# The FFN's up projection as a seven-product block multiplication, with the token axis in quarters

## The chip, the cores and the metric

The kernel runs on one core of one Trainium2 chip. The metric is the device time of one execution in microseconds (us); the profile is one execution of the same program. The engines are named as in the profile: PE (matmuls), PEld (PE's weight loads), DVE (vector), ACT (scalar), POOL (GpSimd) and SP, which issues nearly all DMAs.

## The reference

One encoder layer on T = 1088 tokens (1024 of a prompt, 64 of a sample), model width 1024, FFN width 2816 = 22 x 128, all in float32. Two branches (a gated recurrence and differential attention) are mixed, then comes the FFN; the change lies in the last lines:

```
u = x @ w_in                                     # both branches start from here
...
m   = sigmoid(g_hg) * (y_hg @ w_br_hg) + sigmoid(g_da) * (y_da @ w_br_da)
h   = layer_norm(ALPHA * x + m @ w_out)
up  = h @ w_up                                   # 1024 -> 5632 columns, value | gate
c   = causal depthwise conv3(up) + conv_b        # the state's two rows go in front
val, gate = split(c)
out = layer_norm(ALPHA * h + (silu(gate) * val) @ w_down)
```

## The kernel before

Everything is kept transposed: channels on the 128 partitions, tokens on the free axis. A float32 product is made exactly on PE: each operand is split into a high part (a cast on ACT) and a low part (value minus high part, a subtraction on DVE), and each 128-deep step takes three matmuls, (weight high, token high), (weight high, token low) and (weight low, token high), each with its own weight load. A matmul is named by its token part and its weight part: `mm<-hl,whi` is the second of the three. Tiles of weights (`wraw` by DMA, `whi` from ACT at L68, `wlo` from DVE at L69; 128 x 512 each, that is four 128-deep steps of one 128-column tile) rotate through six buffers in this part of the program.

The stages at the end of the program, in order:

- **br_da** (in `mix`): attention outputs `ydh`/`ydl` times w_br_da; eight column tiles, each over three token chunks (`CHUNKS`, 364, 362 and 362 columns), 24 matmuls per chunk (`proj_chunk`, L84).
- **w_out** (in `mix`): mixed branches `mh`/`ml`, chunk by chunk over eight column tiles. Each chunk's layer norm (`layer_norm`: sums on DVE and POOL, squares on ACT, column sums on PE) follows its eighth tile and gives `hh`/`hl`, the FFN's token operand. `s_r` holds h in DRAM for the residual.
- **up** (in `ffn`, `up_proj`): for each f of the 22, a value tile and a gate tile, each over three chunks of 24 matmuls; ACT copies each result to `u` (L942). After the third chunk a convolution follows: one pass on ACT (L948), two on DVE (L950, L952). Then silu on ACT (L958), value times gate on DVE (L959), and the result goes to DRAM (`s_act`). Its first 256 tokens are also split and kept on chip for all 22 f (`a0h`, `a0l`, L960 and L961). An `order` list starts with chunks 0 and 1 of f = 0 and 1, since chunk 2 of h comes last.
- **down** (in `ffn`): four token chunks (256, 288, 288, 256), eight column tiles each, 66 matmuls per tile (L1016). Chunk 0 takes `a0h`/`a0l`; the others load `s_act` again (`araw`, three buffers) and split it into `ah`/`al` (30 buffers each).

All engines run their instructions in program order; the order between stages is set by the tile framework's scheduler, which places instructions by its own simulation.

Of the kernel before, what the change touches and what calls it, by code (L numbers as in the profile page):

```python
# [10 lines left out]
F32 = mybir.dt.float32  # L11
# [24 lines left out]
CHUNKS = ((0, 364), (364, 362), (726, 362))  # L36
LEVELS = (64, 32, 16)
# [8 lines left out]
class K:  # L46
# [52 lines left out]
    def setup_params(self, cp, pp):  # L99
# [14 lines left out]
        with ExitStack() as es:  # L114
# [34 lines left out]
            # lower bound of the forget gate: softmax over the two rows of logits  # L149
# [18 lines left out]
            # lambda on every partition  # L168
# [55 lines left out]
    def store_x(self, gp):  # L224
        """The sum of the parts is x again, for the residual."""
# [20 lines left out]
    def hgrn(self, h, mm, sc, xs, hp, w0=None):  # L246
# [35 lines left out]
        def lvl(B):  # L282
# [16 lines left out]
            if B == 64:  # L299
                # only the blocks' first halves on the partitions, 32 each  # L300
# [34 lines left out]
        # innermost blocks: one reference in the middle, both signs  # L335
# [18 lines left out]
        # decayed keys and queries at the chunk borders  # L354
# [12 lines left out]
        # states  # L367
# [17 lines left out]
        # outputs  # L385
# [693 lines left out]
```

## Time and profile before

| | |
|---|---|
| time, median of 3 runs (lowest to highest) | 2430.59 us (2429.81 to 2436.18) |
| the profiled execution | span 2430.4 us |
| busy: PE, PEld | 2380.3 us (98%), 2327.2 us (96%) |
| busy: DVE, ACT, POOL | 1379.3 us (57%), 1078.4 us (44%), 385.9 us (16%) |
| chain that ended last, by engine | PE 89%, DMA 3%, DVE 2%, ACT 2% |

How to read it: the span is what the profiler saw from the first to the last instruction; here it agrees with the time to 0.2 us. Busy is the share of the span in which an engine worked. The chain is followed back from the last instruction to whatever released it at each step. Matmul records overlap, since they are pipelined: the pace of PE is read from the starts of successive matmuls, not from the length of one.

### The profile page before, as it was taken

How to read it: one execution, taken by the hardware profiler on the slowest of the kernel's cores; microseconds unless marked ns; L12 is line 12 of the kernel's file. 1: busy time of each engine (PE TensorE's matmuls, PEld its weight loads, DVE VectorE, ACT ScalarE, POOL GpSimd, SP SyncE). 2: the span in 40 equal slices, each digit the busy share in tenths (PEclk: the TensorE clock that was granted, in tenths of full speed). 3: DMA queues.
4: the chain of work that ended last, by engine and by line, in shares of the span. 5: the costliest groups of instructions: out<-in, count | busy, mean ns of one | idle time of the engine just before them, and what ended most of it. 6: DMA issues, size and time to landing. Idle time of an engine off the chain costs nothing.

```text
span 2430.4 us, 40166 instructions
## 1 busy us (share of the span) xinstructions
PE 2380.3 (98%) x15528; PEld 2327.2 (96%) x15528; DVE 1379.3 (57%) x2330; ACT 1078.4 (44%) x2108; POOL 385.9 (16%) x519
## 2 busy tenths in 40 slices
PE   8999999999999999999999999999999999999997
PEld 7999999999999999999999999999999999999997
DVE  3666665554666565565567565874444444456665
ACT  3444444443344344344347543454433333355554
POOL 2222222221521121121120000231000000000100
PEclk9999999999999999999999999999999999999999
DMA  4111111111632332332337674642222121287775
GB/s 126 39 40 47 42 43 48 43 45 54 197 82 79 100 92 70 106 92 70 106 87 235 191 234 143 195 128 73 66 62 65 58 65 58 63 232 226 226 211 157
DMA packets 386278, 260.98 MB, mean 107 GB/s; under 512 B 20667, under 2 KB 375895, under 8 KB 386086
## 3 DMA queue, kind: packets, MB, share of 16 engines
q1 hardware_dynamic: 385574, 258.11, 35.9%
q8 instruction: 122, 2.00, 0.3%
q0 software_dynamic: 512, 0.29, 0.1%
q14 instruction: 70, 0.57, 0.1%
HBM read 191.23 MB, written 54.52 MB: 101 GB/s over the span
## 4 chain that ended last, share of the span: by engine, by line
PE 89%; DMA 3%; DVE 2%; ACT 2%; issue 1%; SPq 0%; POOL 0%; POOLq 0%; DVEq 0%; ACTq 0%
PE mm L84 67%; PE mm L1016 8%; PE s L553 3%; PE av L594 2%; DMA araw<-s_act 2%; PE lv L316 1%; PE wt L588 1%; PE nat L242 1%; DMA gb<-s_g 1%; PE o L399 1%; PE o L402 1%; PE avd L642 1%; PE bs L349 1%; PE U L372 1%; ACT whi L68 1%
## 5 line engine op out<-in xcount | busy, mean ns | idle before, releaser
L84 PE MATMUL mm<-x,whi 128*128 128x362 f32 (+1 forms) x3456 | 878.2, 333 | 6.9 <-ACT x L220 5.5
L84 PEld LDWEIGHTS mm<-x,whi 128*128 128x128 f32 x3456 | 613.5, 190 | 12.6 <-ACT x L220 6.1
L69 DVE TENSOR_TENSOR wlo<-wraw,whi 128x512 fp32r<-128x512 f32 x536 | 371.6, 699 | 431.1 <-ACT whi L68 428.5
L84 PE MATMUL mm<-x,wlo 128*128 128x362 f32 (+1 forms) x1728 | 574.3, 333 | 0.0
L68 ACT CAST whi<-wraw 128x512 fp32r<-128x512 f32 x536 | 320.5, 606 | 410.5 <-PE mm L84 304.5
L84 PE MATMUL mm<-hh,wlo 128*128 128x362 f32 (+1 forms) x1056 | 347.0, 329 | 0.0
L84 PE MATMUL mm<-hh,whi 128*128 128x362 f32 (+1 forms) x1056 | 346.3, 329 | 0.0
L84 PE MATMUL mm<-hl,whi 128*128 128x362 f32 (+1 forms) x1056 | 345.9, 328 | 0.0
L84 PEld LDWEIGHTS mm<-x,wlo 128*128 128x128 f32 x1728 | 327.5, 190 | 1.7 <-issue 1.0
L84 PEld LDWEIGHTS mm<-hl,whi 128*128 128x128 f32 x1056 | 199.2, 189 | 0.1
L84 PEld LDWEIGHTS mm<-hh,whi 128*128 128x128 f32 x1056 | 199.1, 189 | 0.1
L84 PEld LDWEIGHTS mm<-hh,wlo 128*128 128x128 f32 x1056 | 198.9, 188 | 0.0
L1016 PE MATMUL mm<-ah,whi 128*128 128x288 f32 (+1 forms) x528 | 154.3, 293 | 1.0 <-ACT ah L1000 0.9
L1016 PE MATMUL mm<-ah,wlo 128*128 128x288 f32 (+1 forms) x528 | 153.7, 292 | 0.0
L1016 PE MATMUL mm<-al,whi 128*128 128x288 f32 (+1 forms) x528 | 153.3, 291 | 0.1
L942 ACT COPY u<-mm 128x364 f32<-128x364 f32 (+3 forms) x176 | 63.3, 386 | 187.5 <-PE mm L84 187.5
L1016 PEld LDWEIGHTS mm<-ah,whi 128*128 128x128 f32 x528 | 99.2, 188 | 1.7 <-ACT ah L1000 1.5
L1016 PEld LDWEIGHTS mm<-al,whi 128*128 128x128 f32 x528 | 99.4, 188 | 0.3 <-DVE al L1001 0.3
L1016 PEld LDWEIGHTS mm<-ah,wlo 128*128 128x128 f32 x528 | 99.3, 188 | 0.2
L553 PE MATMUL s<-B,A 128*128 128x512 f32 (+3 forms) x384 | 87.7, 354 | 2.3 <-ACT E L574 1.6
L950 DVE SCALAR_TENSOR_TENSOR c<-u,par,c 128x1090 f32<-128x1090 f32 x44 | 59.6, 1355 | 47.3 <-ACT c L948 46.2
L480 POOL TENSOR_TENSOR KL<-kT,B 64x512 fp32r<-64x512 f32 x32 | 49.3, 1540 | 217.9 <-DVE B L479 193.3
(301 smaller groups left out, 4144.7 us busy)
## 6 DMA issues: line engine op xcount, KB each, us to landing
wraw<-w_down SPq DMA_DIRECT2D x160, 256.0 KB, 3.6
wraw<-w_in SPq DMA_DIRECT2D x144, 256.0 KB, 2.9
wraw<-w_up SPq DMA_DIRECT2D x88, 256.0 KB, 2.9
wraw<-w_br_hg SPq DMA_DIRECT2D x48, 256.0 KB, 3.5
wraw<-w_out SPq DMA_DIRECT2D x48, 256.0 KB, 3.1
s_act<-c SPq DMA_DIRECT2D x22, 384.0 KB, 2.3
A<-A SPq DMA_DIRECT2D x64, 128.0 KB, 2.6
araw<-s_act SPq DMA_DIRECT2D x44, 144.0 KB, 3.6
```

The costliest lines, as they stand in the source:

```text
L68: nc.scalar.copy(hi[:, :kn, :], raw[:, :kn, :])
L69: nc.vector.tensor_tensor(lo[:, :kn, :], raw[:, :kn, :], hi[:, :kn, :].bitcast(F32), ALU.subtract)
L84: nc.tensor.matmul(ps[:, :cw], l, r[:, :cw], start=(k == 0 and i == 0), stop=(k == n - 1 and i == 2))
L242: nc.tensor.transpose(ps[:m, i * P:(i + 1) * P], src[:, c * P:c * P + m], self.ident)
L316: nc.tensor.matmul(ps[:m, ch * 64:(ch + 1) * 64], st, mv, start=True, stop=True)
L349: nc.tensor.matmul(ps[:, i, :], X[:, sl], Qp[:, sl], start=True, stop=True)
L480: G.tensor_tensor(kl[r], kT[r, sl], b[r, m, :].bitcast(F32), ALU.subtract)
L553: nc.tensor.matmul(dst[:, kc * 512:kc * 512 + kw], A[i // 2][:, p, m, qc], B[kc][:, m, :kw], start=(p == 0), stop=(p == 1))
L594: self.last_av = nc.tensor.matmul(av[:, i % n4, :], wT[:, kb, :], vn[:, kb, :], start=(kb == 0), stop=(kb == i))
L942: S.copy(u[:, b + off:e + off], ps[:, b - c0:e - c0])
L950: V.scalar_tensor_tensor(c[:, :W - 2], u[:, 1:W - 1], par[:, self.o_w1 + j:self.o_w1 + j + 1], c[:, :W - 2], ALU.mult, ALU.add)
L1016: nc.tensor.matmul(ps[:, :cw], l, r[f][:, :cw], start=(f == 0 and i == 0), stop=(f == NF - 1 and i == 2))
```

## The change

For each f the up projection is one product of a 2 x 2 block matrix of weights (rows: value tile, gate tile; columns: first and second half of the contraction, four 128-deep steps each) and a 2 x 2 block matrix of tokens (rows: the halves of the contraction; columns: two token quarters of 272). It is made with seven block products in place of eight. The token quarters are paired (0, 2) and (1, 3), so each f has two "lanes", c = 0 and c = 1, with 7 x 12 matmuls of 272 columns each. The operands are sums and differences: four of the weights (`wsum`, on POOL) for each f, four of the tokens (t1 to t4) for each pair. Pair 0's token sums are made on POOL; of pair 1's, t1 and t2 on DVE and t3 and t4 on POOL. The products are accumulated in three PSUM banks per lane, and DVE adds them up while it evacuates them. br_da and w_out also run in quarters, w_out pair by pair; for f = 0 and 1, lane 0 of both comes first and lane 1 after it, with the weights made again. Only f = 20 and 21 keep `a0h`/`a0l`; down's chunk 0 loads the other twenty. The rest of the diff renames comments, moves the set-up of `qbd`, sends the last head's attention output through DRAM like the others, and moves pools.

```
     def split_w(self, raw, kn=4):
+        hi, lo = self.wtile("whi", F32R), self.wtile("wlo", F32R)
+        nc.scalar.copy(hi[:, :kn, :], raw[:, :kn, :])
+        nc.vector.tensor_tensor(lo[:, :kn, :], raw[:, :kn, :], hi[:, :kn, :].bitcast(F32), ALU.subtract)
...
+    def seven_weights(self, w, c1, c2, early=False):
...
+        def comb(x, y, op):
+            t = self.wtile("wsum", F32)
+            G.tensor_tensor(t, x, y, op)
+            return t
+        a11 = load(0, c1)
+        yield self.split_w(a11)
+        if early:
+            yield self.split_w(load(4, c1))
+        a21 = load(0, c2)
+        s1 = comb(a21, load(4, c2), ALU.add)
+        yield self.split_w(s1)
+        if early:
+            a11 = load(0, c1)
+        s2 = comb(s1, a11, ALU.subtract)
+        yield self.split_w(s2)
+        a12 = load(4, c1)
+        if not early:
+            yield self.split_w(a12)
+        yield self.split_w(comb(a11, a21, ALU.subtract))
+        yield self.split_w(comb(a12, s2, ALU.subtract))
+        yield self.split_w(load(4, c2))
...
+    def seven_tokens(self, out, za, zb, tile, eng):
...
+        eng.tensor_tensor(t1, b12, b11, ALU.subtract)
+        self.split_tokens(out, "t1", t1, tile)
...
+    def seven_products(self, lanes, tmp, order="1562734"):
...
+            for (gen, x, put), d in zip(lanes, st):
+                w = ws[gen] = ws[gen] if gen in ws else next(gen)
+                bank = {"1": "A", "2": "A", "5": "C", "3": "C"}.get(n, "B")
...
+                if n in "156":
+                    t = d[n] = tmp.tile([P, QW], F32, tag=f"p{n}", name=self.nm("p" + n), bufs=2)
+                    if n == "1":
+                        S.copy(t, ps)
+                    else:
+                        V.tensor_tensor(t, ps, d["1"], ALU.add)
+                    continue
+                row, half, other = {"2": (0, 0, None), "7": (1, 1, "5"), "3": (0, 1, "6"), "4": (1, 0, "1")}[n]
+                for sl, dst in put(row, half):
+                    if other is None:
+                        S.copy(dst, ps[:, sl])
+                    else:
+                        V.tensor_tensor(dst, ps[:, sl], d[other][:, sl], ALU.add)
...
-            self.layer_norm(z, cw, self.o_l1g, self.o_l1b, lnp, zp, CW, ci == 2, done)
+                self.layer_norm([z[k // 4][:, k % 4, :] for k in range(KT)], QW, self.o_l1g, self.o_l1b, lnp, lp,
+                                pi == 1)
...
+            self.xop.append(self.seven_tokens(ops, zz[0], zz[1], optile, V if pi else G))
...
+        for c in range(2):
+            self.seven_products([(weights(f, c == 1), self.xop[c], put(us[f], c)) for f in range(2)], up,
+                                "1256734" if c else "1562734")
...
+        for f in range(2, NF):
+            u, w = new_u(f), weights(f)
+            self.seven_products([(w, self.xop[c], put(u, c)) for c in range(2)], up)
+            conv(f, u)
...
-            if ci == 0:
-                ah, al = a0h, a0l
...
+                if ci == 0 and f >= KEEP:
+                    hi, lo = a0h[f], a0l[f]
+                else:
+                    raw = ap.tile([P, DW], F32, tag="araw", name=self.nm("araw"), bufs=8)
```

The instructions on DVE around one f in the middle of the up projection, before (`wlo` is a weight tile's low part, `c` the convolution's tile, `u` the up projection's result, `a0l` the kept low part):

```order
L950 SCALAR_TENSOR_TENSOR c_17505<-u_17408,par,c_17505 128x1090
L952 SCALAR_TENSOR_TENSOR c_17505<-u_17408,par,c_17505 128x1090
L69 TENSOR_TENSOR wlo_17829<-wraw_17826,whi_17828 128x512
L69 TENSOR_TENSOR wlo_17835<-wraw_17832,whi_17834 128x512
L950 SCALAR_TENSOR_TENSOR c_17605<-u_17408,par,c_17605 128x1090
L952 SCALAR_TENSOR_TENSOR c_17605<-u_17408,par,c_17605 128x1090
L959 TENSOR_TENSOR c_17505<-c_17505,c_17605 128x1090
L961 TENSOR_TENSOR a0l_15941<-c_17505,a0h_15919 128x256
```

The same place with the change, from the last two products of one f to the sixth of the next (`p` is a partial result kept in SBUF, `mm` a PSUM bank; L179 adds a bank and a partial into `u`, L172 makes a partial):

```order
L179 TENSOR_TENSOR u_20515<-mm_20604,p_3090_20541 128x272
L1071 SCALAR_TENSOR_TENSOR c_20766<-u_20515,par,c_20766 128x1090
L179 TENSOR_TENSOR u_20515<-mm_20619,p_3092_20556 128x272
L83 TENSOR_TENSOR wlo_20934<-wsum_20931,whi_20933 128x512
L1073 SCALAR_TENSOR_TENSOR c_20766<-u_20515,par,c_20766 128x1090
L1071 SCALAR_TENSOR_TENSOR c_20772<-u_20515,par,c_20772 128x1090
L83 TENSOR_TENSOR wlo_20967<-wsum_20964,whi_20966 128x512
L1073 SCALAR_TENSOR_TENSOR c_20772<-u_20515,par,c_20772 128x1090
L172 TENSOR_TENSOR p_3137_20846<-mm_20833,p_3128_20806 128x272
L172 TENSOR_TENSOR p_3139_20861<-mm_20848,p_3130_20821 128x272
L83 TENSOR_TENSOR wlo_21000<-wraw_20997,whi_20999 128x512
L172 TENSOR_TENSOR p_3144_20882<-mm_20869,p_3128_20806 128x272
```

DVE now evacuates PSUM between the convolution's passes (before, ACT did all of it), splits seven weight tiles per f where it split four, and the product after next on PE may not write a bank before its L172 has read it.

DVE between w_out and up, before: the end of the last layer norm (`rs` and `dg` are its scale, `z` the normed chunk, `hl` the low parts of the last token operand):

```order
L703 TENSOR_SCALAR rs_15858<-var_15821 128x2
L703 TENSOR_SCALAR rs_15858<-var_15821 106x1
L708 TENSOR_SCALAR dg_15864<-ident,rs_15858 128x128
L708 TENSOR_SCALAR dg_15867<-ident,rs_15858 128x128
L708 TENSOR_SCALAR dg_15870<-ident,rs_15858 106x106
L713 SCALAR_TENSOR_TENSOR z_15488<-z_15488,par,rb_15859 128x362 x8
L899 TENSOR_TENSOR hl_15810<-z_15488,hh_15809 128x362 x8
L69 TENSOR_TENSOR wlo_16273<-wraw_16270,whi_16272 128x512
```

The same place with the change, its end (`z_2211` to `z_2214` are the halves of pair 1's normed quarters; L132 and L138 are token sums, L123 the low parts of the token operands; 20 weight tiles, L83, stand between the last evacuation of w_out and the last of these rows):

```order
L811 SCALAR_TENSOR_TENSOR z_2213_14963<-z_2213_14963,par,rb_16375 128x272 x4
L811 SCALAR_TENSOR_TENSOR z_2214_14964<-z_2214_14964,par,rb_16375 128x272 x4
L132 TENSOR_TENSOR z_2211_14961<-z_2213_14963,z_2211_14961 128x1088
L123 TENSOR_TENSOR t1l_16409<-z_2211_14961,t1h_16408 128x1088
L123 TENSOR_TENSOR b22l_16414<-z_2214_14964,b22h_16413 128x1088
L138 TENSOR_TENSOR z_2214_14964<-z_2214_14964,z_2211_14961 128x1088
L172 TENSOR_TENSOR p_2547_16843<-mm_16830,p_2529_16759 128x272
L123 TENSOR_TENSOR t2l_16419<-z_2214_14964,t2h_16418 128x1088
L83 TENSOR_TENSOR wlo_16943<-wsum_16940,whi_16942 128x512
L172 TENSOR_TENSOR p_2554_16868<-mm_16855,p_2534_16780 128x272
L123 TENSOR_TENSOR t3l_16423<-z_2213_14963,t3h_16422 128x1088
L123 TENSOR_TENSOR t4l_16428<-z_2212_14962,t4h_16427 128x1088
```

Behind the last normed tile there were eight subtractions of 362 columns; now there are two sums and five splits of 1088 columns (two more splits stand further up), in one queue with weight tiles and evacuations.

## Rows read from the trace of the kernel before

**Rows 1.** The page's chain that ended last: shares of the span by engine, by line.

```profile
PE 89%; DMA 3%; DVE 2%; ACT 2%; issue 1%; SPq 0%; POOL 0%; POOLq 0%; DVEq 0%; ACTq 0%
PE mm L84 67%; PE mm L1016 8%; PE s L553 3%; PE av L594 2%; DMA araw<-s_act 2%; PE lv L316 1%; PE wt L588 1%; PE nat L242 1%; DMA gb<-s_g 1%; PE o L399 1%; PE o L402 1%; PE avd L642 1%; PE bs L349 1%; PE U L372 1%; ACT whi L68 1%
```

**Rows 2.** Windows: sum; busy PE, PEld, DVE, ACT, POOL (instructions); PE clock, DMA share, GB/s.

```profile
1600.00:1640.00 40.00, 40.00 (x246) 39.54 (x245) 26.45 (x50) 20.99 (x44) 13.80 (x27) 1.00 0.37 115
1640.00:2129.00 489.00, 489.00 (x2944) 489.00 (x2943) 206.76 (x210) 190.34 (x331) 38.06 (x202) 1.00 0.21 63
```

**Rows 3.** Tile hh: min/median/max ns, first to last start in us, forms.

```profile
L84 PE MATMUL mm<-hh,whi x1056: 323/328/604, 1600.6 to 2129.8; 128*128 128x362 f32 x90, 128*128 128x364 f32 x86
```

**Rows 4.** Timeline of PE in down: start us, length us; 256, then 288 columns.

```profile
2149.83 0.28 PE L1016 MATMUL mm<-a0h,whi 128*128 128x256 f32 x1
2150.90 0.28 PE L1016 MATMUL mm<-a0h,whi 128*128 128x256 f32 x1
...
2299.83 0.29 PE L1016 MATMUL mm<-al,whi 128*128 128x288 f32 x1
2302.88 0.29 PE L1016 MATMUL mm<-ah,whi 128*128 128x288 f32 x1
```

**Rows 5.** Tiles ydh (br_da) and mh (w_out).

```profile
L84 PE MATMUL mm<-ydh,whi x192: 322/328/333, 1406.3 to 1500.6; 128*128 128x362 f32 x128, 128*128 128x364 f32 x64
...
L84 PE MATMUL mm<-mh,whi x192: 324/328/604, 1501.1 to 1600.1; 128*128 128x362 f32 x128, 128*128 128x364 f32 x64
```

**Rows 6.** Lines by form, DVE and ACT: busy us, mean ns | idle before.

```profile
L69 DVE TENSOR_TENSOR wlo<-wraw,whi 128x512 fp32r<-128x512 f32 x504 | 359.3, 717 | 429.3 <-ACT whi L68 426.7 <-PE mm L84 0.6 <-DMA araw<-s_act 0.3
L950 DVE SCALAR_TENSOR_TENSOR c<-u,par,c 128x1090 f32<-128x1090 f32 x44 | 59.6, 1355 | 47.3 <-ACT c L948 46.2 <-DMA wraw<-w_up 1.1
L959 DVE TENSOR_TENSOR c<-c,c 128x1090 f32<-128x1090 f32 x22 | 28.5, 1295 | 24.0 <-ACT c L958 24.0
L659 DVE TENSOR_TENSOR ydl<-ydl,ydh 128x1088 fp32r<-128x1088 f32 x7 | 8.9, 1289 | 1.3 <-ACT ydh L658 1.3
L887 DVE SCALAR_TENSOR_TENSOR z<-g,mm 128x362 f32<-128x362 f32 x16 | 8.4, 524 | 1.8 <-PE mm L84 1.0 <-DMA g<-s_x 0.8
L1001 DVE TENSOR_TENSOR al<-araw,ah 128x256 fp32r<-128x256 f32 x22 | 8.8, 418 | 5.0 <-ACT ah L1000 4.8
...
L68 ACT CAST whi<-wraw 128x512 fp32r<-128x512 f32 x504 | 308.8, 618 | 405.2 <-PE mm L84 303.1 <-PE mm L1016 63.2 <-issue 21.2
```

**Rows 7.** Lines by form, POOL.

```profile
L480 POOL TENSOR_TENSOR KL<-kT,B 64x512 fp32r<-64x512 f32 x32 | 49.3, 1540 | 217.9 <-DVE B L479 193.3 <-DVE smd L625 23.5
```

**Rows 8.** Timeline of POOL and DVE, 618 to 635 us.

```profile
618.62 2.07 POOL L230 TENSOR_TENSOR xf<-x,x 128x364 f32<-128x364 f32 x2 [0.43 <-DMA s_x<-xf]
620.65 3.39 POOL L480 TENSOR_TENSOR KL<-kT,B 64x512 fp32r<-64x512 f32 x2
...
619.84 1.40 DVE L69 TENSOR_TENSOR wlo<-wraw,whi 128x512 fp32r<-128x512 f32 x1 [0.91 <-ACT whi L68]
634.31 0.69 DVE L69 TENSOR_TENSOR wlo<-wraw,whi 128x512 fp32r<-128x512 f32 x1 [7.57 <-ACT whi L68]
```

**Rows 9.** Timeline of DVE after the last chunk of w_out.

```profile
1601.74 0.52 DVE L887 SCALAR_TENSOR_TENSOR z<-g,mm 128x362 f32<-128x362 f32 x1
...
1628.63 2.08 DVE L899 TENSOR_TENSOR hl<-z,hh 128x362 fp32r<-128x362 f32 x4 [0.38 <-POOL hh L898]
```

**Rows 10.** Windows of PE around an earlier pause: busy, clock, DMA share, GB/s.

```profile
552.00:558.00 6.00, 4.51 (x31) 0.79 0.30 87
558.00:564.00 6.00, 6.00 (x31) 0.64 0.00 0
```

**Rows 11.** Tile a0h, and a window of PE in down's chunk 0.

```profile
L1016 PE MATMUL mm<-a0h,whi x176: 274/283/365, 2130.2 to 2203.8; 128*128 128x256 f32 x176
...
2169.00:2179.00 10.00, 7.42 (x63) 1.00 0.86 251
```

**Rows 12.** The page's DMA issues: KB each, median us to landing.

```profile
araw<-s_act SPq DMA_DIRECT2D x44, 144.0 KB, 3.6
```

More of the change, by code (lines that the diff above doesn't have):

```diff
@@ L36 @@
 CHUNKS = ((0, 364), (364, 362), (726, 362))
+QW = T // 4
+QUARTERS = tuple((i * QW, QW) for i in range(4))
+PRODUCTS = {"1": "b11", "2": "b21", "3": "b22", "4": "t4", "5": "t1", "6": "t2", "7": "t3"}
 LEVELS = (64, 32, 16)
@@ new lines, in seven_products @@
+    def seven_products(self, lanes, tmp, order="1562734"):
+        nc = self.nc
+        V, S = nc.vector, nc.scalar
+        st = [{} for _ in lanes]
+        for n in order:
+            xn = PRODUCTS[n]
+            ws = {}
+            for (gen, x, put), d in zip(lanes, st):
+                w = ws[gen] = ws[gen] if gen in ws else next(gen)
+                bank = {"1": "A", "2": "A", "5": "C", "3": "C"}.get(n, "B")
+                first = bank not in d
+                if first:
+                    d[bank] = self.mm.tile([P, 512], F32, tag="mm", name=self.nm("mm"))
+                ps = d[bank][:, :QW]
+                for k in range(4):
+                    (hi, lo), (xh, xl) = w[k], x[xn][k]
+                    for i, (l, r) in enumerate(((hi, xh), (hi, xl), (lo, xh))):
+                        nc.tensor.matmul(ps, l, r, start=(first and k == 0 and i == 0), stop=(k == 3 and i == 2),
+                                         skip_group_check=not first)
+                if n in "156":
[11 more added lines that the diff above has]
+                        V.tensor_tensor(dst, ps[:, sl], d[other][:, sl], ALU.add)
@@ L921, in ffn @@
[L921 to L932 removed]
+        cst = self.a0p.tile([P, 4, 44], F32, name="cst")
@@ new lines, in ffn, with new_u @@
+        a0h = {f: self.a0p.tile([P, C0], F32R, name=f"a0h{f}") for f in range(KEEP, NF)}
+        a0l = {f: self.a0p.tile([P, C0], F32R, name=f"a0l{f}") for f in range(KEEP, NF)}
+        up = self.up
+        cp = self.ux.enter_context(tc.tile_pool(name="upc", bufs=1, side="right", reuse_waits="tile"))
+        W = T + 4
+        def new_u(f):
+            u = up.tile([P, 2, W], F32, tag="u", name=self.nm("u"), bufs=2)
+            for i in range(2):
+                j = f + i * NF
+                G.memset(u[:, i, 0:2], 0.0)
@@ L952, in up_proj, with put, f @@
-            V.scalar_tensor_tensor(c[:, :W - 2], u[:, 2:W], par[:, self.o_w2 + j:self.o_w2 + j + 1],
-                                   c[:, :W - 2], ALU.mult, ALU.add)
-            cs[j] = c
-        def act(f):
-            val, gate = cs[f], cs[f + NF]
+            return u
+        def put(u, c):
+            def f(row, half):
+                t0 = (2 * half + c) * QW
+                for s0, s1, off in ((0, TP, 2), (TP, T, 4)):
+                    b, e = max(s0, t0), min(s1, t0 + QW)
+                    if b < e:
+                        yield slice(b - t0, e - t0), u[:, row, b + off:e + off]
+            return f
@@ L964, in act @@
             nc.sync.dma_start(self.s_act[row, TP:T], val[:, TP + 2:W - 2])
-        order = [(0, 0, 0), (0, 0, 1), (0, 1, 0), (0, 1, 1), (1, 0, 0), (1, 0, 1), (0, 0, 2), (0, 1, 2), (1, 0, 2)]
-        order += [(1, 1, ci) for ci in range(3)]
-        order += [(f, which, ci) for f in range(2, NF) for which in range(2) for ci in range(3)]
-        for f, which, ci in order:
-            up_proj(f, which, ci)
-            if which == 1 and ci == 2:
-                act(f)
-        ux.close()
+        us = [new_u(f) for f in range(2)]
```

319 lines of the change are left out of this document (168 added, 151 removed).

## The prediction

> **What bounds the kernel now.** I first read the chain of the work that ended last [rows 1]: 89% of it is PE, and 67% of the span is one line, the matmuls of all projections. Then I cut the end of the program into windows [rows 2]. In the up projection PE is busy for 489.00 of 489.00 us at clock 1.00, while DVE works 206.76 and ACT 190.34: the stage costs what its matmuls cost, and DVE has 58% to spare. Third, the tile view [rows 3] gives the stage's ends: 1600.6 to 2129.8, 529.2 us for 3 x 1056 = 3168 matmuls. So a change that takes matmuls away is paid out in full, as long as nothing else becomes late. The window 1600 to 1640 shows what is hidden there today: PE is busy in all of its 40.00 us, though DVE finishes the layer norm of the last chunk in it.
>
> **The matmuls of the up projection.** Per f there were 2 tiles x 3 chunks x 24 = 144 matmuls of about 362 columns; now there are 7 products x 2 lanes x 12 = 168 of 272, in all 22 x 168 = 3696. No row has 272 columns, so I bound its pace. In down [rows 4], 9 steps of 256 columns take 2150.90 − 2149.83 = 1.07 us, 0.1189 each; 23 steps of 288 columns take 2302.88 − 2299.83 = 3.05 us, 0.1326. 272 lies halfway: 0.1258 us (bounds 0.1189 and 0.1326, that is ±25 us over the stage if the pace were a step function, which the two rows give no sign of). 3696 x 0.1258 = 465.0 us, **−64.2**. An f takes 168 x 0.1258 = 21.1 us of PE.
>
> The Trainium skill, TensorE: Matmul & The Clock Gate, section "Wait — 56ns, not 53.3ns?", says that successive warm matmuls of N columns start N ÷ 2.4 GHz + about 2.5 ns apart, which would be 115.8 ns at 272 columns and 428 us for the stage. At 256 columns it would be 109.2 ns, and the row shows 118.9, so I go by the rows.
>
> **br_da and w_out.** 576 matmuls each become 8 x 4 x 24 = 768 of 272 columns: 96.6 us against 94.7 (1406.3 to 1501.0) and 99.3 (1501.1 to 1600.4) [rows 5]. The layer norm's column sums are made four times in place of three, about 2 us more; and the last head's output now takes the way through DRAM, so br_da's last operand is late by some 1.5 us. Sum: **+4** (0 to +8).
>
> **The hand-off from w_out to up.** This is the term I am least sure of. Before, DVE's chain from the last evacuation to the last low part ran from 1601.74 to 1630.71, 29 us [rows 9], behind the `order` list's matmuls. Now DVE works off, in program order and behind the last evacuation of w_out: 20 weight splits of 0.717, 10 token splits and 2 token sums of 1088 columns at 1.289, some 50 operations of 272 columns at about 0.43 (between 0.418 for 256 and 0.524 for 362), and ten small ones, 2 us [rows 6]: 14.3 + 15.5 + 21.5 + 2 = 53 us. POOL makes 16 weight sums and the last of the token sums at the same time, and a DVE operation with two inputs from SBUF takes twice as long beside POOL: 1.40 us beside [rows 8], 0.69 alone. If a quarter of the 30 us of such operations is met, +8: the last token operand t4 is there after 61 us, t2 after about 57. PE has lane 0 of f = 0 and 1 and then lane 1 to do, 336 matmuls or 42.3 us, of which the last 4 products of two f (6, 7, 3 and 4; 96 matmuls, 12.1 us) need t2 or what follows it. They end at 57.3 + 12.1 = 69.4, 27 us late. After such a pause PE runs at half clock for some time: in the one that the trace has at 552 us the windows lose 6 x 0.21 + 6 x 0.36 = 3.4 us [rows 10]. Sum: **+30**. Bounds: 5, if the chain is hidden as now; 50, if every operation with two SBUF inputs is doubled. I take the middle since the queue's content is counted and only POOL's share is a guess.
>
> **DVE and POOL in the middle of up.** This edit I cost at nothing. DVE's work per f: 7 weight splits x 0.717, 4 convolution passes (two lines) x 1.355, 1.295 for the multiplication [rows 6], and 12 evacuations of 272 columns or parts of them, 4.6: 16.3 of 21.1 us. ACT: 7 casts x 0.618 and three passes over 1090 columns with four evacuations, about 10. POOL: 4 sums; the nearest row, 64 x 512 [rows 7], says 1.54 each, 6.2 per f. The place where it is tight is the sixth product's evacuation (L172): bank B may not be written by the seventh product before, and the convolution's passes of the f before stand ahead of it on DVE. Adding these up from the end of the previous f's fourth product: lane 0's evacuation is done 8.1 us after it, lane 1's at 9.9; PE comes back to the bank at 12.1 and 13.6. Slack 3.7 to 4.0 us. If POOL and DVE halve each other while both run, DVE loses about 3 us of its 6.2 beside POOL and has 19.4 per f: still covered. What it costs if that cover is gone is the second rival.
>
> **The start of down.** Before, chunk 0's operands were on chip; now 20 of 22 come from `s_act` through eight buffers, each landing 3.6 us after its issue [rows 12], with ACT's casts queued behind weight casts that wait for the last matmuls, and DVE's splits between the last convolution's passes: +6 us at the start. Chunk 0 lost time before: 2130.2 to 2203.8 [rows 11] for 8 x 66 matmuls, 62.8 us by the pace above; 10 us went to windows such as 2169 to 2179, where PE worked 7.42 of 10 us under a DMA share of 0.86, weights and 30 prefetched operands of the next chunk together. Now only ten of these are prefetched (the buffers are shared with chunk 0): −6. The other operands of chunk 1 come later: +2. Sum: **+2** (−6 to +10).
>
> **Sum.** The profiled execution takes 2430.4, the median is 2430.6. 2430.6 − 64.2 + 4 + 30 + 2 = 2402.4; rounded, with a little for the seventh weight tile per f, 2403.
>
> **The rivals.**
>
> *The hand-off is hidden after all*, since DVE runs ahead of the order that I read (waits on POOL and ACT are short): the term is 5, the time 2378. For it: the same stretch costs nothing today; against it: 53 us of counted work against 42.
>
> *POOL's sums block DVE*, the other side. If a POOL sum keeps DVE from its second input for its whole length, DVE needs 16.3 + 6.2 = 22.5 us per f, 1.4 over PE's 21.1, in 20 f +28 us: 2431, no change. From there it decides. A POOL sum on 128 partitions of 512 columns may be slower than the row; at 2.0 us DVE's f is 24.3, +64 us, 2466. For it: the DVE split beside POOL that took 1.40 in place of 0.69 is a doubling, and DVE's queue stalls PE in its order, not on the average. Against it: that split lay inside 5.46 us of uninterrupted POOL work (2.07 + 3.39) [rows 8] and still ended after 1.40, so POOL does not shut it out for as long as it is busy. The Trainium skill, SBUF — State Buffer, section "SBUF: two separate sides", has the port pair that DVE and GpSimd share as an exclusive lock, held for a whole instruction while the other blocks. By that rule DVE loses up to the 6.2 us per f; the trace agrees in the doubled split, and shows no case of a longer wait.
>
> *DVE is late in part*: the slack of 4 us is used up by POOL in a part of the f, 1 us each on average, +20 on top of the forecast: 2423.
>
> *Matmuls of 272 columns go as fast as those of 256*: at 0.1189 up gains another 3696 x 0.0069 = 25 us and the two stages before it 2 x 768 x 0.0069 = 11, so 2367. That the pace rose by 13.7 ns for 32 columns between the two rows [rows 4] speaks against a step just there. By the rule of the Trainium skill cited above (TensorE: Matmul & The Clock Gate) it would be 37 and 15 us.
>
> **How the numbers follow.** Forecast, 2390 to 2418: 0.52. Hand-off hidden, 2372 to 2390: 0.15. Late in part, 2418 to 2440: 0.15. POOL blocks DVE, from 2431 to beyond 2466: 0.14. Pace of 256 columns, below 2372: 0.04. The range 2374 to 2442 leaves out the last, a bit of the second and most of the fourth. A measurement can tell about 0.3%, 7.3 us, from no change: faster is below 2423.3, slower above 2437.9. Faster: 0.52 + 0.15 + 0.04 + a third of the late cases = 0.76. Same: the rest of these, 0.09. Slower: 0.15.
>
> **What would show it.** Up should start at about 1605 and have one pause of 20 to 30 us on PE near 1650, with the releaser on DVE (t2, t3 or t4), and clock 0.5 behind it; after it f should follow f every 21.1 us with PE busy throughout and matmuls starting 0.126 us apart. If windows in the middle of up show PE at less than 95% with waits on DVE, the second or third rival holds; the length of a weight split beside a POOL sum says which, and the POOL sum's own length (1.54 assumed) how much. If no pause is seen near 1650, the first does. Down should begin with a pause of about 6 us on ACT's or DVE's splits. The prediction is wrong if DVE's evacuations, not the matmuls, set the pace of an f.

## The result, and the profile after

The changed kernel takes 2417.77 us (median of 4 runs, 2413.59 to 2419.98) against 2433.11 us for the kernel before, in 4 runs (2429.81 to 2436.18): a ratio of 0.9938, 95% interval 0.9919 to 0.9956. That is faster by 0.6%, 15 us above the 2403 of the forecast and inside its range of 2374 to 2442, which also held "no change". The profiled execution took 2417.09 us, with a span of 2415.3.

The tiles give the ends of the stages, first with the change, then before. The columns are those of [rows 3]: min/median/max ns, first to last start.

```profile
L192 PE MATMUL mm<-ydh,whi x256: 282/288/395, 1404.9 to 1504.1; 128*128 128x272 f32 x128
L192 PE MATMUL mm<-mh,wlo x256: 285/288/492, 1504.7 to 1604.8; 128*128 128x272 f32 x128
L165 PE MATMUL mm<-t4h,wlo x176: 285/289/292, 1640.6 to 2116.6; 128*128 128x272 f32 x176
```

```profile
L84 PE MATMUL mm<-mh,wlo x192: 322/328/417, 1501.5 to 1600.4; 128*128 128x362 f32 x128, 128*128 128x364 f32 x64
L84 PE MATMUL mm<-hh,wlo x1056: 322/328/334, 1600.9 to 2130.1; 128*128 128x362 f32 x89, 128*128 128x364 f32 x87
```

w_out ends at 1604.8, where before it was 1600.4; up ends at 2116.6, where before it was 2130.1. Up's 529.7 us have become 511.8, the two stages ahead cost 4.4 more, and what follows up takes 298.7 us where it took 300.3: −17.9 + 4.4 − 1.6 = −15.1, the difference of the spans.

The windows of the stretch (columns as in [rows 2]) show where the rest of the 64 us went:

```profile
1600.00:1620.00 20.00, 16.85 (x120) 15.78 (x118) 18.89 (x20) 10.19 (x18) 12.98 (x7) 1.00 0.17 53
1620.00:1640.00 20.00, 18.66 (x114) 17.51 (x115) 16.98 (x33) 8.84 (x20) 8.35 (x8) 0.83 0.32 93
1640.00:1660.00 20.00, 13.40 (x93) 12.73 (x91) 17.19 (x29) 11.27 (x24) 10.30 (x10) 0.83 0.48 147
1660.00:1680.00 20.00, 9.92 (x44) 8.87 (x44) 15.45 (x20) 10.55 (x17) 9.56 (x5) 0.71 0.27 86
1680.00:1700.00 20.00, 19.86 (x149) 19.49 (x149) 19.64 (x26) 10.14 (x15) 15.08 (x15) 0.95 0.41 117
...
1800.00:1900.00 100.00, 100.00 (x797) 100.00 (x796) 78.44 (x114) 44.35 (x68) 43.42 (x65) 1.00 0.30 91
```

From 1740 on PE is busy throughout, 797 matmuls in 100 us or 0.1255 us each, with DVE at 78%. At that pace the 3696 matmuls are worth 463.7 us; 511.8 − 463.7 = 48.1 us are lost, nearly all between 1605 and 1740. Only 44 matmuls start between 1660 and 1680, where a full window of that length has 160, and the granted clock is 0.71. The page's chain shows the same shift: PE has 85% where it had 89% [rows 1], DVE 4% where it had 2%.

```profile
PE 85%; DVE 4%; DMA 4%; ACT 2%; issue 2%; POOL 1%; SPq 0%; POOLq 0%; DVEq 0%; ACTq 0%
```

PE stands still for 22.3 us between 1600 and 1745. The six longest entries in the list of its waits (us in total, times, longest) are:

```profile
PE mm L165 <- ACT t1h L122: 6.0, 1, 6.0
PE var L795 <- POOL acc L791: 3.8, 1, 3.8
PE mm L165 <- ACT whi L82: 3.5, 2, 2.0
PE mm L165 <- DVE t2l L123: 2.1, 1, 2.1
PE mm L165 <- ACT b11h L122: 1.5, 1, 1.5
PE mm L165 <- ACT t2h L122: 1.4, 1, 1.4
```

So there are many short pauses and no long one: first for lane 0's weights (`whi`, near 1620), then for a layer norm (`acc`), for t1 and for t2.

The timeline of DVE holds the length of the hand-off (start, length, idle time ahead and its releaser):

```profile
1608.99 0.42 DVE L1001 SCALAR_TENSOR_TENSOR z<-g,mm 128x272 f32<-128x272 f32 x1
...
1671.61 1.29 DVE L138 TENSOR_TENSOR z<-z,z 128x1088 f32<-128x1088 f32 x1 [2.40 <-POOL z L135]
1672.81 0.43 DVE L172 TENSOR_TENSOR p<-mm,p 128x272 f32<-128x272 f32 x1
1674.06 2.55 DVE L123 TENSOR_TENSOR t2l<-z,t2h 128x1088 fp32r<-128x1088 f32 x1 [0.81 <-ACT t2h L122]
```

The first row is the last evacuation of w_out and ends 4.6 us after the start of w_out's last matmul; the last row ends at 1676.6 and is what the remaining four products of f = 0 and 1 in lane 1 need (t2). That is 67.2 us; the forecast had 57.3.

### The profile page after: what moved, and what is told of

The parts are those of the page before. It is cut to its first block, busy times and chain, and to the rows that moved or that the text cites. A ratio compares the mean times of both kernels' runs of the same rounds, so it can differ in the third digit from the quotient of the medians.

```text
span 2415.3 us, 42919 instructions
## 1 busy us (share of the span) xinstructions
PE 2342.9 (97%) x16486; PEld 2284.5 (95%) x16486; DVE 1555.6 (64%) x2700; ACT 1101.4 (46%) x2124; POOL 567.9 (24%) x608
## 3 DMA queue, kind: packets, MB, share of 16 engines
q10 hardware_dynamic: 4224, 4.46, 0.5%
q8 instruction: 129, 2.11, 0.4%
## 4 chain that ended last, share of the span: by engine, by line
PE 85%; DVE 4%; DMA 4%; ACT 2%; issue 2%; POOL 1%; SPq 0%; POOLq 0%; DVEq 0%; ACTq 0%
PE mm L192 45%; PE mm L165 17%; PE mm L1139 9%; PE s L655 3%; PE av L696 2%; PE wt L690 1%; PE lv L418 1%; DVE wlo L83 1%; DMA araw<-s_act 1%; PE nat L344 1%; DMA gb<-s_g 1%; PE o L501 1%; DMA ydl<-s_yd 1%; PE o L504 1%; PE avd L741 1%
## 5 line engine op out<-in xcount | busy, mean ns | idle before, releaser
L83 DVE TENSOR_TENSOR wlo<-wraw,whi 128x512 fp32r<-128x512 f32 x504 | 360.7, 721 | 259.0 <-ACT whi L82 252.5
L1139 PE MATMUL mm<-ah,whi 128*128 128x288 f32 (+1 forms) x688 | 199.8, 291 | 3.4 <-ACT ah L1123 2.3
L1139 PE MATMUL mm<-al,whi 128*128 128x288 f32 (+1 forms) x688 | 199.0, 290 | 1.7 <-DVE al L1124 1.7
L1139 PE MATMUL mm<-ah,wlo 128*128 128x288 f32 (+1 forms) x688 | 199.3, 291 | 0.3 <-DVE wlo L83 0.3
L82 ACT CAST whi<-wsum 128x512 fp32r<-128x512 f32 x96 | 59.5, 619 | 101.1 <-PE mm L165 92.9
L100 POOL TENSOR_TENSOR wsum<-wraw,wraw 128x512 f32<-128x512 f32 x48 | 82.7, 1723 | 68.8 <-DVE wlo L83 51.0
L83 DVE TENSOR_TENSOR wlo<-wsum,whi 128x512 fp32r<-128x512 f32 x96 | 74.3, 774 | 32.1 <-ACT whi L82 30.7
L179 DVE TENSOR_TENSOR u<-mm,p 128x272 f32<-128x272 f32 (+2 forms) x176 | 60.5, 366 | 50.2 <-PE mm L165 50.2
L398 POOL TENSOR_TENSOR P<-X,k 128x544 f32<-128x544 f32 (+1 forms) x32 | 60.3, 1886 | 122.7 <-ACT X L392 76.3
L691 ACT COPY wT<-wt 128x512 f32<-128x512 f32 (+1 forms) x96 | 46.4, 483 | 81.7 <-PE wt L690 81.1
L696 PE MATMUL av<-dvn,wT 128*128 128x128 f32 x576 | 80.1, 275 | 0.6 <-ACT wT L691 0.6
```

The source lines that it names most:

```text
L100: G.tensor_tensor(t, x, y, op)
L179: V.tensor_tensor(dst, ps[:, sl], d[other][:, sl], ALU.add)
L398: G.tensor_tensor(pk, xv[:, :, :hb], blocks(k, B)[:, :, :hb], ALU.mult)
L691: S.copy(wT[:, g * 4:g * 4 + nb, :], ps[:, :nb * P].rearrange("p (n e) -> p n e", e=P))
L696: self.last_av = nc.tensor.matmul(av[:, i % n4, :], wT[:, kb, :], vn[:, kb, :], start=(kb == 0), stop=(kb == i))
L1139: nc.tensor.matmul(ps[:, :cw], l, r[f][:, :cw], start=(f == 0 and i == 0), stop=(f == NF - 1 and i == 2))
```

## The experiments

The loss behind w_out is the length of up, from the last start of `mm<-mh,wlo` to the last start of `mm<-t4h,wlo`, less 463.7 us. Three explanations were put against each other. **Queue**: the amount of DVE's work behind w_out sets the loss. **Chain**: the operands of pair 1 wait for each other, for the store into `s_r` and for POOL. **Lock**: a DVE operation with two SBUF inputs waits for the POOL operation that it meets. All times are medians of 4 or 5 runs; the other columns read the profiled execution of each kernel, which for e9 is 6 us and for e12 4.5 us above the median and for the others within 3 us of it. br_da, ahead of everything that the experiments edit, starts between 1402.4 and 1410.4 in these executions, so the loss compares kernels better than the time does. The kernel before took 2430.5 to 2434.8 us (medians) beside the experiments; the ratios are to the runs of the same session.

| kernel | time, us | ratio to before, 95% | w_out ends | last evacuation ends | t2 low part ends | up ends | loss |
|---|---|---|---|---|---|---|---|
| the change | 2417.8 | 0.9919 to 0.9956 | 1604.8 | 1609.4 | 1676.6 | 2116.6 | 48.1 |
| e1 t2 over t1 | 2417.3 | 0.9923 to 0.9963 | 1603.1 | 1612.2 | 1676.0 | 2116.0 | 49.2 |
| e2 token sums on DVE | 2409.0 | 0.9889 to 0.9922 | 1603.8 | 1606.8 | 1667.5 | 2107.3 | 39.8 |
| e3 eight plain products | 2454.8 | 1.0078 to 1.0108 | 1603.7 | 1604.5 | none | 2152.0 | 18.2 |
| e4 POOL's sums twice | 2422.3 | 0.9944 to 0.9982 | 1605.0 | 1610.2 | 1677.8 | 2121.6 | 52.9 |
| e5 both | 2408.1 | 0.9875 to 0.9909 | 1606.1 | 1609.9 | 1669.7 | 2109.2 | 39.4 |
| e6 no sums on POOL | 2411.0 | 0.9886 to 0.9919 | 1606.2 | 1608.2 | 1673.2 | 2109.3 | 39.4 |
| e7 quarter 1, then 3 | 2422.0 | 0.9936 to 0.9966 | 1612.6 | 1617.5 | 1681.1 | 2120.6 | 44.3 |
| e8 = e6 + e7 | 2408.0 | 0.9875 to 0.9905 | 1615.1 | 1619.7 | 1672.2 | 2108.4 | 29.6 |
| e12 all quarters in turn | 2406.9 | 0.9881 to 0.9914 | 1617.2 | 1621.5 | 1673.4 | 2109.8 | 28.9 |
| e10 weights once | 2414.1 | 0.9915 to 0.9952 | 1605.6 | 1610.6 | 1678.1 | 2111.4 | 42.1 |
| e9 lane 1 with pair 0 | 2412.8 | 0.9911 to 0.9948 | 1609.5 | 1614.1 | 1707.6 | 2117.2 | 44.0 |
| e11 = e9 + e10 | 2403.6 | 0.9872 to 0.9903 | 1605.1 | 1610.0 | 1691.3 | 2101.4 | 32.6 |

(e3 has 4224 matmuls in up and ends it with `mm<-b3h,wlo`; 530.1 us are taken off there.)

**e1, the sum t2 ahead of t3 and over t1.**

```diff
-        t3 = b12
-        G.tensor_tensor(t3, b22, b12, ALU.subtract)
         self.split_tokens(out, "b22", b22, tile)
-        t2 = b22
+        t2 = t1
         eng.tensor_tensor(t2, b22, t1, ALU.subtract)
         self.split_tokens(out, "t2", t2, tile)
+        t3 = b12
+        G.tensor_tensor(t3, b22, b12, ALU.subtract)
```

> The sum t2 is written over t1 and made before t3, so that it waits neither for the store of h into s_r nor for POOL's sum t3. Theory 'queue' (the amount of DVE's work behind the last evacuation of w_out, with what POOL's work beside it adds, sets the loss of 48 us between 1605 and 1740): that work is unchanged, so within 3 us of the changed kernel's 2417. Theory 'chain' (the token operands of pair 1 wait for each other, for the store of 4.9 us and for POOL's t3 of 3.2 us, while DVE waits too): t2 comes 6 to 8 us earlier, and the time is 2409 to 2412.

Measured: 2417.3, nothing gained, the number of "queue"; but the timelines of POOL and DVE show a different reason:

```profile
1668.27 2.82 POOL L139 TENSOR_TENSOR z<-z,z 128x1088 f32<-128x1088 f32 x1 [6.43 <-DMA s_r<-z]
...
1668.64 3.60 DVE L136 TENSOR_TENSOR z<-z,z 128x1088 f32<-128x1088 f32 x1
```

t2 no longer waits for the store or for t3, and starts 65.5 us after w_out's end (66.8 in the change). But now it meets POOL's t3 and takes 3.60 us in place of 1.29: it ends at 1672.24, where POOL's end (1671.09) and its own 1.29 give 1672.38. One wait has taken the place of another.

**e2, all token sums on DVE**: the engine argument becomes `V` for both pairs, and t3 and t4 use it too.

```diff
-            self.xop.append(self.seven_tokens(ops, zz[0], zz[1], optile, V if pi else G))
+            self.xop.append(self.seven_tokens(ops, zz[0], zz[1], optile, V))
```

> All eight token sums on DVE, where six were on POOL. Queue: six more operations of 1.29 us stand in DVE's queue, 8 us in all, at least 3 of them behind the last evacuation: 2420 to 2425. Chain: a sum takes 1.3 us on DVE in place of 2.5 to 3.6 on POOL, on the way to t2, t3 and t4 of both pairs: 3 to 8 us less, 2409 to 2414.

Measured: 2409.0, 9 us less, the number of "chain", and the loss fell by 8.3, although DVE got six sums more. Counted work alone is refuted. From the last evacuation to the end of t2's split DVE is busy for 51.89 us, where in the change, with fewer sums, it was 56.54 (its row stands at e9; columns as in [rows 2]):

```profile
1606.80:1667.50 60.70, 45.12 (x299) 41.96 (x297) 51.89 (x92) 34.66 (x69) 22.61 (x20) 0.89 0.37 115
```

What DVE does beside POOL's token sums takes longer: the split of pair 0's t1 took 2.60 us in the change, with such a sum under way, and 1.28 here. So the 9 us do not tell "chain" from "lock".

**e5** does both edits:

> All token sums on DVE, and t2 written over t1 before t3 is made. In the run with the sums on DVE (2409) DVE still stood for 3.0 us at t3, whose target must first be stored into s_r; here t1's split, b22's and t2 come first. Chain: 3 to 4 us less than 2409, 2405. Queue: the same work, 2409 within 3.

Measured: 2408.1 and a loss of 39.4, the number of "queue"; the order of the sums adds nothing that can be told from e2.

**e3, eight plain products**: quarters, pairs and layer norms stay, all sums go, and the weights are loaded as before.

```diff
...
-            self.seven_products([(w, self.xop[c], put(u, c)) for c in range(2)], up)
...
+            for i in range(2):
+                w = wts(f, i)
+                for q in (0, 2, 1, 3):
+                    plain(f, i, u, w, q)
```

> The same quarters, pairs and layer norms, but the up projection as eight plain products: no sums of weights or tokens, 8 token splits per pair in place of 14, 4 weight splits per f in place of 7, ACT evacuates; 4224 matmuls in place of 3696. PE's own work grows by 528 x 0.1255 = 66 us. If the sums and splits of the seven products make the loss at the hand-off (queue and chain alike), the loss falls from 48 to about 15 us or less: 2450 or below. If the layer norm of a pair behind the last w_out product makes it, it stays above 35 us: 2470 to 2485.

Measured: 2454.8 us, slower than before (by 0.8 to 1.1%). Up ends at 2152.0, 548.3 us after w_out; 4224 x 0.1255 = 530.1, so the loss is 18.2, near the 15 of the first reading, though its 2450 is missed by 5. The one pause left is small:

```profile
1640.00:1660.00 20.00, 15.50 (x106) 15.21 (x105) 10.16 (x19) 11.04 (x22) 1.25 (x4) 0.83 0.33 105
```

So the seven products save 66 us of matmuls and pay 30 of them at the hand-off; the layer norm behind quarters alone is not the loss. The 30 are for sums, splits and evacuations together, since e3 also gives the evacuations to ACT.

**e4, POOL's sums twice from f = 4 on.**

```diff
             G.tensor_tensor(t, x, y, op)
+            if again:
+                G.tensor_tensor(t, x, y, op)
```

> From f = 4 on POOL makes each of its four weight sums twice (the second time over the first, same values). The rival of the prediction that POOL shuts DVE out: DVE's 16.5 us per f grow by up to 4 x 1.72 = 6.9 to 23.4, 2.3 over PE's 21.1, so 18 x 2.3 = 41 us more, 2458. If DVE loses only a part while POOL works beside it, DVE stays below 21 us per f and the time within 3 us of 2417.

Measured: 2422.3 (0.9944 to 0.9982 of before), some 4 us more: 2 us beyond the "within 3" of the second reading, and 36 short of the rival's 2458. In the middle of up:

```profile
1720.00:1740.00 20.00, 17.07 (x124) 16.86 (x123) 17.20 (x22) 8.26 (x14) 15.68 (x19) 0.91 0.33 109
...
1800.00:1900.00 100.00, 100.00 (x798) 100.00 (x797) 92.65 (x114) 44.02 (x66) 81.13 (x89) 1.00 0.28 85
```

For the same 114 instructions DVE takes 92.65 us where it took 78.44, per f 19.5 where it took 16.5: four POOL sums more cost DVE 3.0 us, 0.75 each (0.71 over 15 whole f, in the rows at e6). PE stays busy throughout; the 4 us went where the doubling sets in, at 1720.

**e6, the weight sums on DVE as well** (with e5): `G.tensor_tensor(t, x, y, op)` becomes `nc.vector.tensor_tensor(t, x, y, op)`.

> As the kernel with all token sums on DVE and t2 before t3, and the weight sums on DVE as well, so that POOL makes no sum of the seven products. Theory 'lock' (a DVE operation with two SBUF inputs that meets a POOL operation waits until that one ends; in the middle of up a POOL sum costs DVE 0.75 us in the mean, by the run with the sums twice: 19.5 against 16.5 us per f): a sum on DVE costs 0.69 us, so DVE's time per f stays at 16.3 us, and the hand-off loses less because no split waits for POOL: 3 to 8 us less than with the weight sums on POOL, 2398 to 2404. Queue by counted work alone: 12 more sums of 0.69 on DVE before up's products of f = 0 and 1 are done, 8 us more: 2412 or above.

Measured: 2411.0, between the two numbers and so a miss for both; the loss stays at 39.4. In the middle of up PE stays busy. DVE needs 260.60 us for 15 f, that is 17.4 per f and not 16.3 (the change, e4, e6; columns as in [rows 2]):

```profile
1760.00:2076.50 316.50, 316.50 (x2518) 316.50 (x2517) 246.84 (x361) 139.10 (x209) 137.28 (x211) 1.00 0.29 90
...
1760.00:2076.50 316.50, 316.50 (x2519) 316.50 (x2518) 289.37 (x360) 137.42 (x210) 256.56 (x271) 1.00 0.29 90
...
1760.00:2076.50 316.50, 316.50 (x2519) 316.50 (x2518) 260.60 (x420) 139.08 (x211) 39.02 (x150) 1.00 0.30 90
```

Sixty sums of 0.69 us on DVE add 13.8 us to its time, 0.23 each: on POOL a sum had cost DVE about two thirds of what it costs on DVE itself. The 0.75 of e4 holds for sums added to four others, not for these four. Against e5, t2 comes 3.4 us later behind w_out's end (67.0 for 63.6), and what follows it is as much shorter: for the weight sums gain and cost cancel, as far as this shows.

**e7, quarter 1 of w_out ahead of quarter 3.**

```diff
...
+                for q, z in qz:
+                    wout([(q, z)])
+                    norm(q, z)
```

> Only the order of w_out is changed: of pair 1, quarter 1 is finished with its layer norm begun before quarter 3 starts (w_out's weights are loaded and split once more, 16 tiles). Queue and chain: one of two layer norms, about 12 to 15 us of DVE's queue behind the last evacuation, and b11 and b21 with it, move under 24 us of matmuls: 10 to 18 us less than the changed kernel, 2400 to 2408. If the weight tiles made twice for f = 0 and 1 are what is late, nothing is gained: 2415 or more.

Measured: 2422.0, no faster than the change (the intervals overlap); a miss for "queue" and "chain", and the number of the third reading, though for another reason. The loss fell by 4, but w_out grew from 100.1 to 106.7 us: quarter 1's column sums and variances on PE, some 5 us, now stand in it, and PE waited 1.5 us for a weight tile. And behind w_out PE stood for 6.9 us at a matmul of quarter 1's layer norm, which now stands ahead of the products in its order (timelines of PE, DVE and POOL):

```profile
1625.65 0.76 PE L808 MATMUL rb<-dg,ones 128*128 128x128 f32 x2 [6.92 <-DVE dg L807]
...
1620.04 5.66 DVE L807 TENSOR_SCALAR dg<-ident,rs 128x128 f32<-128x128 f32 x2 [0.60 <-POOL rs L803]
...
1620.51 1.25 POOL L100 TENSOR_TENSOR wsum<-wsum,wraw 128x512 f32<-128x512 f32 x1
1621.72 2.47 POOL L142 TENSOR_TENSOR z<-z,z 128x1088 f32<-128x1088 f32 x1
1624.16 1.25 POOL L100 TENSOR_TENSOR wsum<-wsum,wraw 128x512 f32<-128x512 f32 x1
```

A `dg` takes 0.27 us in the median; one of these two took 5.46. DVE stood in it while POOL ran three sums one behind the other, and was done 0.3 us after the third (1625.70 and 1625.41). This is "lock" in its longest case, and here the operation read one tensor and a column of factors, not two tensors.

**e8, e6 and e7 together.**

> Both together: quarter 1 of w_out ahead of quarter 3, and no sum on POOL. If the two parts of the loss are separate, the gains add up: 12 to 25 us below the changed kernel, about 2390 to 2398. If both only clear the same wait (the weights are late behind it), no more than 3 us better than the better one of the two.

Measured: 2408.0. With no sums on POOL, the wait for `dg` is 0.2 us where it was 6.9. Against e6 the loss fell by 9.8 to 29.6, but w_out is 4.9 longer and starts 4.0 later, of which 3.0 are there at br_da's start already. In time 3.0 us are left, the number of the second reading; the loss says that both parts moved.

**e9, lane 1 of f = 0 and 1 with pair 0's operands** (`self.xop[0]` for `self.xop[c]`).

> Lane 1 of f = 0 and 1 multiplies pair 0's token operands again (so this part of the result is not the reference's); pair 1's operands are still made, by the same instructions, but first needed at f = 2, some 21 us of matmuls later. Chain (the loss is the wait for pair 1's operands): 15 to 21 us less than the changed kernel's 2417, 2396 to 2402. Queue (DVE has the same work to do before f = 3 whoever waits for it): the wait turns up at weights or at f = 2, and less than 8 us is gained: 2410 or more.

Measured: 2412.8, and 4 us of the loss. With 21 us more time, t2 came 98.1 us after w_out's end in place of 71.8. The windows from the last evacuation to the end of t2's split, first of e9, then of the change:

```profile
1614.10:1707.57 93.47, 74.03 (x504) 69.60 (x502) 84.22 (x126) 50.32 (x93) 58.20 (x48) 0.89 0.37 112
```

```profile
1609.41:1676.61 67.20, 46.09 (x290) 42.78 (x288) 56.54 (x90) 35.91 (x70) 32.60 (x24) 0.84 0.34 104
```

DVE is busy for 90% and 84% of these stretches. It filled the time with the weights and evacuations that PE asked for earlier, and pair 1's operands went to the end of the queue. "Chain" alone is refuted.

**e10, one weight tile per f in lane 1 of f = 0 and 1.**

```diff
+        def one(f):
...
+            w = self.split_w(t)
+            while True:
+                yield w
```

> In lane 1 of f = 0 and 1 one weight tile per f serves all seven products (so this part of the result is not the reference's): 12 weight splits on DVE and ACT, 8 sums on POOL and 10 loads fall away around the hand-off; the tokens are as in the changed kernel. Queue: 12 x 0.72 + 8 x 0.75 = 15 us of DVE's time are gone, and with them 10 to 15 us: 2402 to 2407. Chain: the operands of pair 1 come when the layer norm and the sums let them, and no more than 5 us is gained: 2412 or more.

Measured: 2414.1, 3.7 us less, and a loss of 42.1, 6 us less: the number of "chain". t2 is not earlier (72.5 us after w_out's end, 71.8 in the change); what was gained lies behind it. **e11** does both:

> Both together: lane 1 of f = 0 and 1 waits neither for pair 1's tokens nor for weights made again. If tokens and weights together are the loss of 48 us, the loss falls below 20 us: 2389 or less. If the gains of the two runs overlap (the one wait hides the other), it is more than their sum. If over 25 us of loss are left, it is something else, the layer norm's matmuls, the clock, or pair 0's operands.

Measured: 2403.6, a loss of 32.6: 15.5 us, more than 4.1 + 6.0. The two waits hide each other, but over 25 us are left, which the expectation gave to something else.

**e12, all four quarters in turn** (with e8).

> As the kernel with quarter 1 ahead of quarter 3 and no sums on POOL (2408), but pair 0 too is made quarter by quarter, so that quarter 0's layer norm and splits can start 25 us earlier, in the time in which DVE is only 60% busy under w_out's matmuls; w_out's weights are loaded once more, 16 tiles. Queue: some 12 to 15 us of DVE's work leave the stretch behind w_out, the loss there falls from 30 to about 20 us, w_out costs up to 5 more: 2398 to 2405. If the wait is the path from the last quarter's evacuation on (layer norm, sums, splits), which this does not touch, the loss behind w_out stays within 4 us of 30 and the time is 2408 to 2415.

Measured: 2406.9, the loss 28.9, within 4 of e8's as the second reading had it. DVE is busier under w_out, 80.02 us between 1500 and 1600 against 65.12 in e8, but some 11 us of that are the 16 weight tiles split once more. From the last evacuation to t2 (first e12, then e8) its work fell by 3.6 us and not by 12 to 15, and t2 came only 0.9 us earlier behind w_out's end:

```profile
1621.45:1673.40 51.95, 39.07 (x256) 36.22 (x256) 46.37 (x89) 29.37 (x57) 6.52 (x7) 0.92 0.43 130
```

```profile
1619.70:1672.19 52.49, 39.88 (x256) 35.80 (x256) 49.94 (x92) 32.62 (x60) 7.71 (x7) 0.90 0.40 117
```

**What the table says together.** In the five kernels with the weight sums on POOL where nothing else is left out (the change, e1, e2, e5, e7) the loss is the time from w_out's end to t2's low part, less 24 us: 71.8 and 48.1, 72.9 and 49.2, 63.7 and 39.8, 63.6 and 39.4, 68.5 and 44.3. With these sums on DVE it is that time less 27.5 (e6, e8, e12: 67.0 and 39.4, 57.1 and 29.6, 56.2 and 28.9). So in these eight kernels the loss follows the arrival of pair 1's t2: what moved t2 against w_out's end moved the loss, and the time with it where w_out did not grow (it did in e7, e8 and e12). That t2 is not the only wait is shown by e9 and e11. Of the 336 matmuls of f = 0 and 1 (42.2 us) 96 (12.0 us) come behind t2: with nothing lost behind t2 the loss would be t2's time less 30.1. So some 6 us are lost behind t2 with weight sums on POOL and some 3 without; in e10, where the last products wait for no new weights, nothing is (72.5 and 42.1).

What t2 waits for is mostly DVE's queue: on its way DVE is busy for 84% in the change, and for 95% in e8 (49.94 of 52.49 us). But the work alone does not set it: in e12 some 3.6 us of it are gone, and idle time takes most of their place (46.37 of 51.95 us).

## Why the prediction was right, and where it was off

**The matmuls.** 0.1258 us was worked out, 0.1255 measured; −64.2 became 463.7 − 529.7 = −66.0. The halfway point between 256 and 288 columns holds. The 115.8 ns that the prediction worked out by the Trainium skill, TensorE: Matmul & The Clock Gate, section "Wait — 56ns, not 53.3ns?", are not what these matmuls take, each of which comes with a weight load of its own: they start 125.5 ns apart.

**br_da and w_out.** +4 forecast, +4.4 measured, in part by luck: the terms listed (+1.9, −2.7, +2 and +1.5) add up to 2.7, and it was br_da that grew by 4.9 us from first to last start, w_out by 1.2.

**DVE and POOL in the middle of up.** Right: no cost. 16.5 us per f where 16.3 was counted and 19.4 was feared, and PE at 100%. The rival on the other side is refuted twice, by these windows and by e4: even with the sums made twice DVE has 19.5 of 21.1 us. A sum of two loaded tiles takes POOL 1.72 us in the mean, not 1.54 (page, columns as in [rows 6]):

```profile
L100 POOL TENSOR_TENSOR wsum<-wraw,wraw 128x512 f32<-128x512 f32 x48 | 82.7, 1723 | 68.8 <-DVE wlo L83 51.0
L83 DVE TENSOR_TENSOR wlo<-wsum,whi 128x512 fp32r<-128x512 f32 x96 | 74.3, 774 | 32.1 <-ACT whi L82 30.7
```

**The start of down.** +6 at the start was forecast. PE stood for 2.11 and 1.46 us behind ACT's and DVE's splits, then ran at half clock for some 3 us (0.54 granted from 2122 to 2125): about 5. All that follows up came out at −1.6, where +2 was forecast.

```profile
2119.24 0.39 PE L1139 MATMUL mm<-ah,whi 128*128 128x256 f32 x1 [2.11 <-ACT ah L1123]
2121.09 0.39 PE L1139 MATMUL mm<-al,whi 128*128 128x256 f32 x1 [1.46 <-DVE al L1124]
```

**The hand-off** is the term that was mis-sized: +30 (5 to 50), measured 48.1. Its mechanism was right in the main: DVE's queue up to t2's split, then 12 us of products. The step that failed is "They end at 57.3 + 12.1 = 69.4". Counted from the end of w_out, t2 was there after 71.8 us. 4.6 of the 14.5 us missing are w_out's last evacuation, which the prediction put at the end of the matmuls; it stood behind pair 0's splits, held up by POOL's sums. The rest is idle time of DVE: 67.2 − 56.54 = 10.7 us, spread over waits for POOL's t3, ACT's casts and the layer norm. The prediction gave DVE's queue no idle time: it took every operand to be there when its turn came. Behind t2 some 6 us were lost where 3.4 were forecast.

That DVE's busy time up to t2, 56.5 us, came out so near the 57.3 is luck. Held against e8, where POOL makes no sums, the operations on this way are some 11 us longer (the 20 weight splits alone take 18.9 us in place of 13.3), where 8 was forecast; the work itself was counted some 4 us too high. And the sign that the prediction named, one pause of 20 to 30 us on PE, was not seen: PE stood for 22.3 us in short pauses, the longest for ACT's cast of t1. In the total, too, errors offset each other: the hand-off's +18 met −1.8 of the matmuls and −3.6 behind up.

That POOL's work lengthens DVE's was right, but the argument against the lock was wrong. A split that ended after 1.40 us within 5.46 us of POOL's work [rows 8] does not show that POOL doesn't shut DVE out; this one got its turn between two POOL operations. Others did not. The prediction says that the trace before shows no longer wait, but it has a split of 1.90 us, with POOL at work beside it:

```profile
648.29 1.90 DVE L69 TENSOR_TENSOR wlo<-wraw,whi 128x512 fp32r<-128x512 f32 x1 [0.18 <-ACT whi L68]
```

In e1 the whole 2.45 us that were left of one POOL operation were waited for, and in e7 three operations in a row. The Trainium skill, SBUF — State Buffer, section "SBUF: two separate sides", has it so: the loser blocks for the whole of the instruction under way; the trace agrees, with 3.60 us for an operation of 1.29 in e1. The three in a row of e7 go beyond that.

What is left when lane 1 waits neither for t2 nor for new weights (e11's 32.6 us) is told by windows that begin about w_out's end, in the change, e11 and e3 (columns as in [rows 2]):

```profile
1604.90:1740.00 135.10, 112.42 (x771) 107.15 (x771) 122.30 (x174) 67.66 (x115) 74.89 (x75) 0.90 0.34 103
...
1604.90:1740.00 135.10, 122.87 (x895) 118.15 (x894) 121.90 (x179) 66.45 (x112) 67.45 (x77) 0.96 0.28 87
...
1604.90:1740.00 135.10, 130.60 (x1004) 128.97 (x1003) 69.11 (x101) 63.16 (x124) 17.82 (x52) 0.97 0.29 88
```

PE is idle for 22.7, 12.2 and 4.5 us of them. The layer norms' own matmuls, which the prediction left out of PE's 42.3 us, take 12.6, 12.6 and 10.9. The missing clock is worth 13.5, 5.4 and 4.1 us, an estimate made as the prediction made it at 552 us. Together that is 48.8, 30.2 and 19.5, close to the losses of 48.1, 32.6 and 18.2. e11's idle time is waits for weight tiles (5.9 us, 5.0 of them for lane 0's near 1620, as in the change) and for evacuations of PSUM (6.2).

What stays open is how much of this could be hidden: whether a longer stretch of PE work that needs neither pair 1 nor new weights would hide the wait was not tried.

## What to carry to other kernels

An algorithm that trades matmuls for additions paid, here, where its operands are first made, and not where it runs: price that place as a queue, from the last result that it needs to the first product that uses it, with the idle time of the engine in between. An addition moved to POOL relieved DVE by a third of its length in the middle of up (0.23 of 0.69 us), where DVE had time to spare; at the hand-off, where PE waits for DVE, the six token sums were cheaper on DVE (9 us less), and the weight sums made no difference that can be told. A wait that is taken away from an operation in a full queue is worth nothing until what it meets next is known (e1, e7).

## What the runs showed of the hardware

DVE and POOL: an operation with two SBUF inputs that started while POOL ran one ended when POOL had ended plus its own length (e1: 1672.24 against 1671.09 + 1.29). An operation can be shut out for several of POOL's in a row: a `dg` of 0.27 us took 5.46 beside three (e7). At DVE's load in the middle of up a weight sum takes DVE 0.69 us; made on POOL, it still cost DVE about two thirds of that (e6 against the change), and a sum more on POOL, of 1.3 to 2.2 us, cost DVE 0.71 (e4). PE: matmuls of 272 columns with a weight load each start 0.1255 us apart at full clock, as the line between 256 and 288 columns had it.
